# Eight byte offsets for the split halves of the expert blocks in a PEER encoder block

## The chip, the core and the metric

The kernel runs on one core of a Trainium2 chip. Its time is the device time of one execution, in microseconds (us). Five engines work side by side, each through its own instructions in order: TensorE (PE in the rows; PEld is its loading of the stationary operand), VectorE (DVE), ScalarE (ACT), GpSimd (POOL) and SyncE (SP), which here only issues transfers. Transfers (DMA) are issued from the queues of SyncE, ScalarE and GpSimd and are carried by 16 DMA engines. SBUF is the on-chip memory: 128 partitions, each a row of bytes, in which a tile has a start and a length.

## The reference

One encoder layer on 512 tokens of width 1024. The part that matters is the expert stage, in which each token picks 16 of 16384 experts for each of 8 heads, and an expert adds its row of `expert_v`, weighted by a gate and by gelu of its row of `expert_u` times the token:

```python
def peer_block(xb, w_q, sub_keys, expert_u, expert_v):
    T = xb.shape[0]
    q = (xb @ w_q).reshape(T, PEER_HEADS, 2, PEER_HALF)
    s = jnp.einsum('thpd,hpkd->thpk', q, sub_keys)
    sv, si = lax.top_k(s, PEER_TOPK)
...
    top_s, pos = lax.top_k(cand, PEER_TOPK)
    eidx = jnp.take_along_axis(cidx, pos, axis=-1)
    gate = jax.nn.softmax(top_s.astype(jnp.float32), axis=-1).astype(xb.dtype)
    u = jnp.take(expert_u, eidx, axis=0)
    act = jax.nn.gelu(jnp.einsum('thkd,td->thk', u, xb))
    v = jnp.take(expert_v, eidx, axis=0)
    return jnp.einsum('thk,thkd->td', gate * act, v)
```

Before it stands a mixer (input projection, a three-tap convolution and window means, output projection), behind it a gate with a per-layer embedding and the last norm.

## The kernel before

Tokens are handled as four tiles of 128. For three of them (384 tokens) the experts are not gathered but computed densely: all 16384 experts are streamed as 128 blocks of 128, for u and for v. For the fourth tile the chosen rows are gathered one at a time by GpSimd (`fetch`) and worked on by VectorE (lines 559 and 563).

Float32 operands are split in two, since TensorE takes each operand in a rounded 4-byte form (float32r): the high half is the value rounded, the low half is the rest, and a product is three matmuls, high by high, low by high, high by low (`mm3_pair`, lines 126, 128, 130). For a streamed block:

- `u_dma` / `v_dma` (lines 577, 595, SyncE) load 512 KB into `uraw` or `vraw`;
- `u_h` / `v_h` (lines 583, 601, ScalarE) write the high half `uH` or `vH`, `u_l` / `v_l` (589, 607, VectorE) the low half `uL` or `vL`; each of the four names has three buffers of 128 x 1024;
- `score` takes uH and uL as the stationary operand, in 8 slices of 128 columns, against 384 token columns: 24 matmuls a block;
- `mix` takes vH and vL as the moving operand, 512 columns at a time, and the mixing weights `wH` and `wL` (gate times gelu, written by lines 688 and 693 for two blocks at once, in two buffers each) as the stationary one: 18 matmuls a block, into accumulators that stand through all blocks.

The program has three parts in a row. First the mixer and the scores for the top-k. Then 76 blocks of u are scored, while VectorE picks the experts and makes the gate matrix by one-hot products; ScalarE collects that in the tile `stage` (two buffers of 13312 bytes a partition) and stores it to memory from its own queue (line 484), twelve stores of 1664 KB; there a scheduler sets the order of instructions. Last, from about 646 us, comes the mixing, in an order written out by hand: v blocks are mixed in turn, eight of them straight away, then in turn with the 52 blocks of u that are left, then alone. Each engine runs that order; a wait on another engine or on a transfer is put where a tile is first written over bytes that an earlier tile still holds, or is first read. In the mixing, the pools on the left of SBUF lie behind one another: `ub` (uraw, uH, uL), `vb` (vraw, vH, vL), `wq` (the gelu tiles, wH, wL). Pools of the part before lie in the same bytes, `stage` among them.

Of the kernel before, what the change touches and what calls it, by code (L numbers as in the profile page):

```python
# [8 lines left out]
F32R = mybir.dt.float32r  # L9
# [7 lines left out]
P = 128  # L17
T = 512
NT = T // P
D = 1024  # L20
DC = D // P
# [27 lines left out]
GGB = 2  # L49
URB = 2  # L50
G_START = 10
G_RATE1 = 0.7
RATES = (1.5, 3.2, 2.9)
MAIN_ORDER = ((ND, 0, 99), (0, 0, 99), (1, 0, 99), (2, 0, 99))
# [6 lines left out]
def block_kernel(ctx: ExitStack, tc: tile.TileContext, x, pT_in, g_cols, w_in, conv_w, pool_w,  # L61
# [262 lines left out]
    ub = sbx.enter_context(tc.tile_pool(name="ub", reuse_waits="tile", bufs=3))  # L324
# [176 lines left out]
    for hd in range(H):  # L501
# [11 lines left out]
        for tp in range(2):  # L513
            ps = psum.tile([P, T], F32, name="tp", bufs=2)
            for ti in range(2):
                for b in range(2):
                    t = 2 * tp + ti
                    o = (2 * ti + b) * P
# [29 lines left out]
    def gather(n=1, pin=False):  # L548
        for _ in range(n):
            k = done[0]  # L550
            if k >= 2 * P:
                return
            done[0] += 1
            for kk in range(k, min(k + AHEAD_G, 2 * P)):
                if kk not in rows:
                    rows[kk] = fetch(u_rows if kk < P else v_rows, kk % P)
            g = rows[k]
            if k < P:
                ins = nc.vector.scalar_tensor_tensor(g, g, 1.0, xrow, op0=OP.mult, op1=OP.mult,  # L559
                                                     accum_out=act[:, k:k + 1])  # L560
            else:
                accg = accs["g"]
                ins = nc.vector.scalar_tensor_tensor(accg, g, gate3[:, k - P:k - P + 1], accg, op0=OP.mult,  # L563
                                                     op1=OP.add)
            if pin:
                tc.keep_in_program_order(ins)
            if k == P - 1:
                nc.sync.dma_start(xrow, h_d[ND])
                nc.scalar.activation(act, act, AF.Gelu_apprx_tanh)
                nc.vector.tensor_tensor(gate3, gate3, act, op=OP.mult)  # L570

    ublk, vblk, wblk = {}, {}, {}

    def u_dma(i):
        if i < NE:
            raw = ub.tile([P, DC, P], F32, name="uraw", bufs=URB)
            nc.sync.dma_start(raw, u_blk[i])
            ublk[i] = [raw, None, None]

    def u_h(i):  # L580
        if i < NE:
            ublk[i][1] = ub.tile([P, DC, P], F32R, name="uH")
            nc.scalar.activation(ublk[i][1], ublk[i][0], AF.Copy)  # L583

    def u_l(i):
        if i < NE:
            raw, uh, _ = ublk[i]
            ublk[i][2] = ub.tile([P, DC, P], F32R, name="uL")
            nc.vector.tensor_tensor(ublk[i][2], raw, uh.bitcast(F32), op=OP.subtract)  # L589

    def v_dma(n):
# [5 lines left out]

    def v_h(n):
        if n < NE:
            vblk[n][1] = vb.tile([P, D], F32R, name="vH")  # L600
            nc.scalar.activation(vblk[n][1], vblk[n][0], AF.Copy)  # L601

    def v_l(n):
        if n < NE:
            raw, vh, _ = vblk[n]
            vblk[n][2] = vb.tile([P, D], F32R, name="vL")
            nc.vector.tensor_tensor(vblk[n][2], raw, vh.bitcast(F32), op=OP.subtract)  # L607

    def score(ps, i):
# [11 lines left out]
    def prep_u(i):  # L621
        u_dma(i)
        with tc.high_priority(AHEAD):
            u_h(i)
            u_l(i)
# [3 lines left out]
    for i in range(NB):  # L629
# [9 lines left out]
        while mi < len(main) and spent < (i + 1) * total_m / (NB - SLACK):  # L639
            spent += main[mi][0]  # L640
            main[mi][1]()
            mi += 1
        gather(max(0, int((i + 1 - G_START) * G_RATE1) - done[0]), True)
    phg.close()
# [4 lines left out]
    vb = vs.enter_context(tc.tile_pool(name="vb", reuse_waits="tile", bufs=3))  # L649
# [116 lines left out]
    for n in range(3):  # L766
        v_dma(n)
    u_dma(NB + 2)
    u_dma(NB + 3)
    new_quad(0)  # L770
    if NR % 4 == 0:
        new_quad(NR // 4)
    for n in range(2):
        v_h(n)
        w_mult(n)
        w_h(n)
        v_l(n)
        w_l(n)
        v_dma(n + 3)
    heldU = {}  # L780
    for m in range(PRE):
        heldU[m] = acts(NR + m)
        if m == 0:
            for t in range(ND):
                acc[t] = [psum.tile([P, T], F32, name="o%d%d" % (t, hf)) for hf in range(2)]
        u_h(NB + m + 2)
        u_l(NB + m + 2)
        u_dma(NB + m + 4)
        gelu(NR + m, heldU[m])
    LAST = 3  # L790
    left = None
    for n in range(NE - LAST):
        m = n + LAG
        i = n - NS
# [28 lines left out]
        if fu:  # L823
            ps = acts(m)
            u_h(u_of(m) + 2)
# [3 lines left out]
        if fu:  # L829
            u_l(u_of(m) + 2)  # L830
            u_dma(u_of(m) + 4)
        v_h(n + 2)
        if not fu and m < NE:
            w_h(m)
        gather(q >= 2)
        v_l(n + 2)
        v_dma(n + 5)
        if not fu and m < NE:
# [8 lines left out]
        if n == NE - LAST - 1:  # L847
            for k in range(n + LAG + 1, NE):
                w_mult(k)
                w_h(k)  # L850
                w_l(k)
            for k in range(n + 3, NE):
                v_h(k)
                v_l(k)
            tail_norm(ND)
# [145 lines left out]
```

## Time and profile before

| what | us |
|---|---|
| median of three runs | 1451.63 (1448.16 to 1456.77) |
| the profiled execution | 1445.91 |
| its span | 1444.1 |
| TensorE busy | 1423.6 |
| VectorE busy | 1137.7 |
| ScalarE busy | 614.2 |
| GpSimd busy | 383.2 |

The span runs from the first instruction to the last; 1.8 us lie around it. A matmul's busy time overlaps with its neighbour's, so what one costs is read from when they start. Times in the views are counted from the start of the span. An idle time is put down to what ended it.

### The profile page before, as it was taken

The page shows a single profiled execution, that of the slowest core. Times are in us where ns is not written, and L with a number is a line of the kernel's source. Part 1 is how long each engine was busy: PE and PEld are TensorE (multiplying, and loading weights), DVE is VectorE, ACT ScalarE, POOL GpSimd, SP SyncE. Part 2 cuts the span into 40 slices and gives each one's busy share as a digit, 9 for nine tenths or more (in the row PEclk, how much of TensorE's full clock was granted, in tenths as well). Part 3 has the DMA queues.
Part 4 walks back from the last instruction along what each step waited for, and adds up shares of the span by engine and source line. Part 5 has one row for each costly group of instructions (what it writes and reads, how often), then busy time and mean ns, then how long its engine had stood idle before and what let it go on. Part 6 is the DMA issues. An engine that isn't in the chain of part 4 may idle for free.

```text
span 1444.1 us, 20600 instructions
## 1 busy us (share of the span) xinstructions
PE 1423.6 (99%) x7785; PEld 1272.1 (88%) x7785; DVE 1137.7 (79%) x2078; ACT 614.2 (43%) x864; POOL 383.2 (27%) x260
## 2 busy tenths in 40 slices
PE   7999999999998999999999999999999999999997
PEld 5789888999998999998999999999998888888886
DVE  5653579899998997879988778888877777776765
ACT  5321533344564675764333333333332334343345
POOL 0000000002221231125866555444443112332000
PEclk9999999999998999999999999999999999999999
DMA  8233630157788898889998989998987899998621
GB/s 303 88 109 96 235 116 30 34 193 277 226 280 269 286 323 309 281 304 342 390 346 324 374 327 341 348 341 326 342 335 269 320 339 339 339 340 331 249 72 73
DMA packets 152083, 381.38 MB, mean 264 GB/s; under 512 B 10928, under 2 KB 72112, under 8 KB 151728
## 3 DMA queue, kind: packets, MB, share of 16 engines
q1 hardware_dynamic: 72400, 211.75, 40.9%
q0 software_dynamic: 36864, 134.23, 25.4%
q10 hardware_dynamic: 42720, 34.08, 7.0%
q8 instruction: 61, 1.00, 0.3%
q14 instruction: 38, 0.31, 0.1%
HBM read 339.92 MB, written 40.11 MB: 263 GB/s over the span
## 4 chain that ended last, share of the span: by engine, by line
PE 79%; DVE 11%; DMA 6%; ACT 2%; issue 2%; ACTq 0%; SPq 0%; DVEq 0%
PE o L130 11%; PE o L126 11%; PE o L128 11%; PE acc L126 9%; PE acc L130 9%; PE acc L128 9%; PE u L130 5%; PE u L126 5%; PE u L128 5%; DMA uraw<-in_u_blk 3%; DMA tH<-in_w_gate 3%; DVE uL L589 2%; DVE vL L607 1%; PE g L473 1%; PE g L474 1%
## 5 line engine op out<-in xcount | busy, mean ns | idle before, releaser
L539 POOL DMA_INDIRECT gr<-in_u_rows,eidx x128 | 199.5, 1558 | 648.3 <-DVE tsm L393 329.6
L539 POOL DMA_INDIRECT gr<-in_v_rows,eidx x128 | 183.5, 1433 | 289.6 <-DVE xrow L563 278.9
L126 PE MATMUL o<-vH,wH 128*128 128x512 f32 x768 | 237.5, 390 | 0.0
L130 PE MATMUL o<-vH,wL 128*128 128x512 f32 x768 | 237.3, 390 | 0.1
L128 PE MATMUL o<-vL,wH 128*128 128x512 f32 x768 | 236.9, 390 | 0.0
L601 ACT ACTIVATE vH<-vraw 128x1024 fp32r<-128x1024 f32 x128 | 135.5, 1059 | 220.8 <-PE o L130 163.7
L126 PE MATMUL acc<-xH,uH 128*128 128x384 f32 x608 | 206.6, 340 | 3.0 <-ACT uH L583 3.0
L607 DVE TENSOR_TENSOR vL<-vraw,vH 128x1024 fp32r<-128x1024 f32 x128 | 156.2, 1220 | 65.9 <-ACT vH L601 65.9
L128 PE MATMUL acc<-xL,uH 128*128 128x384 f32 x608 | 206.7, 340 | 0.0
L130 PE MATMUL acc<-xH,uL 128*128 128x384 f32 x608 | 204.5, 338 | 0.0
L589 DVE TENSOR_TENSOR uL<-uraw,uH 128x1024 fp32r<-128x1024 f32 x128 | 155.6, 1217 | 25.2 <-ACT uH L583 25.0
L583 ACT ACTIVATE uH<-uraw 128x1024 fp32r<-128x1024 f32 x128 | 135.3, 1058 | 91.4 <-DMA uraw<-in_u_blk 48.8
L130 PEld LDWEIGHTS o<-vH,wL 128*128 128x128 f32 x768 | 144.0, 188 | 31.1 <-DVE wL L693 0.8
L128 PEld LDWEIGHTS o<-vL,wH 128*128 128x128 f32 x768 | 144.2, 188 | 30.8
L563 DVE SCALAR_TENSOR_TENSOR xrow<-gr,gate,xrow 128x1024 f32<-128x1024 f32 x128 | 164.1, 1282 | 5.3 <-DMA xrow<-h_d 4.8
L126 PEld LDWEIGHTS o<-vH,wH 128*128 128x128 f32 x768 | 143.4, 188 | 26.6
L559 DVE SCALAR_TENSOR_TENSOR gr<-gr,xrow 128x1024 f32<-128x1024 f32 x128 | 154.2, 1217 | 2.4 <-DMA gr<-in_u_rows,eidx 2.3
L130 PE MATMUL u<-xH,uL 128*128 128x384 f32 x416 | 139.6, 336 | 0.0
L126 PE MATMUL u<-xH,uH 128*128 128x384 f32 x416 | 139.5, 335 | 0.0
L128 PE MATMUL u<-xL,uH 128*128 128x384 f32 x416 | 139.3, 335 | 0.0
L126 PEld LDWEIGHTS acc<-xH,uH 128*128 128x128 f32 x608 | 115.4, 190 | 3.9 <-ACT uH L583 3.9
L128 PEld LDWEIGHTS acc<-xL,uH 128*128 128x128 f32 x608 | 115.5, 190 | 0.0
(214 smaller groups left out, 2330.7 us busy)
## 6 DMA issues: line engine op xcount, KB each, us to landing
uraw<-in_u_blk SPq DMA_DIRECT2D x128, 512.0 KB, 4.9
vraw<-in_v_rows SPq DMA_DIRECT2D x128, 512.0 KB, 5.8
G_d<-stage ACTq DMA_DIRECT2D x12, 1664.0 KB, 10.4
gq<-G_d SPq DMA_DIRECT2D x26, 768.0 KB, 6.9
A_d<-a ACTq DMA_DIRECT2D x17, 768.0 KB, 5.4
aq<-A_d SPq DMA_DIRECT2D x17, 768.0 KB, 9.3
wraw<-in_w_in SPq DMA_DIRECT2D x8, 1024.0 KB, 5.6
wraw<-in_w_q SPq DMA_DIRECT2D x8, 1024.0 KB, 5.6
```

Of the source, the lines that this page charges most:

```text
L126: nc.tensor.matmul(ps, lh, rh, start=start, stop=False)
L128: nc.tensor.matmul(ps, lh, rl, start=False, stop=False)
L130: nc.tensor.matmul(ps, ll, rh, start=False, stop=stop)
L473: nc.tensor.matmul(o, oh[:, 1, n, :, e], gg[:, 0, n, :, e], start=True, stop=False)
L474: nc.tensor.matmul(o, oh[:, 1, n, :, e], gg[:, 1, n, :, e], start=False, stop=True)
L539: nc.gpsimd.indirect_dma_start(out=g, out_offset=None, in_=table, in_offset=bass.IndirectOffsetOnAxis(ap=eidx[:, k:k + 1], axis=0))
L559: ins = nc.vector.scalar_tensor_tensor(g, g, 1.0, xrow, op0=OP.mult, op1=OP.mult, accum_out=act[:, k:k + 1])
L563: ins = nc.vector.scalar_tensor_tensor(accg, g, gate3[:, k - P:k - P + 1], accg, op0=OP.mult, op1=OP.add)
L583: nc.scalar.activation(ublk[i][1], ublk[i][0], AF.Copy)
L589: nc.vector.tensor_tensor(ublk[i][2], raw, uh.bitcast(F32), op=OP.subtract)
L601: nc.scalar.activation(vblk[n][1], vblk[n][0], AF.Copy)
L607: nc.vector.tensor_tensor(vblk[n][2], raw, vh.bitcast(F32), op=OP.subtract)
```

## The change

Each high and low half of a streamed block becomes a tile of 1024 + 32 elements, of which 1024 are used, from an element that goes by the block's number modulo eight: 0, 1, 2, 4, 8, 12, 16, 24 elements, which are 0, 4, 8, 16, 32, 48, 64 and 96 bytes. Blocks have 128 numbers, so each offset has 16 of them, for u and for v. The loaded blocks (uraw, vraw) and the other tiles start at their pool's usual places.

```diff
+OFFS = (0, 1, 2, 4, 8, 12, 16, 24)
...
+    def moved(pool, name, k):
+        o = OFFS[k % len(OFFS)]
+        return pool.tile([P, D + 32], F32R, name=name)[:, o:o + D]
...
-            ublk[i][1] = ub.tile([P, DC, P], F32R, name="uH")
+            ublk[i][1] = moved(ub, "uH", i).rearrange("p (c n) -> p c n", c=DC)
...
-            ublk[i][2] = ub.tile([P, DC, P], F32R, name="uL")
+            ublk[i][2] = moved(ub, "uL", i).rearrange("p (c n) -> p c n", c=DC)
...
-            vblk[n][1] = vb.tile([P, D], F32R, name="vH")
+            vblk[n][1] = moved(vb, "vH", n)
...
-            vblk[n][2] = vb.tile([P, D], F32R, name="vL")
+            vblk[n][2] = moved(vb, "vL", n)
```

A half's tile has 4224 bytes a partition instead of 4096. There are six such tiles in `ub` and six in `vb`, so `vb` begins 768 bytes further on, and `wq` behind it 1536. The first buffer of wL lay in bytes 137216 to 140288 of a partition, which is the end of the first buffer of `stage` (126976 to 140288); now it lies in 138752 to 141824, across the end of the first and the start of the second (140288 to 153600).

All engines have the same instructions in the same order, and all waits are the same but for two rows of VectorE, at the start of the mixing. Before, they read as follows: the low half of v's first block, the first wL (`a_6386` is the tile of gelu values), the low halves of another block of v and of two blocks of u, a product of gelu and gate, a gather's dot product, and the next vL and wL.

```order
L607 TENSOR_TENSOR vL<-vraw,vH 128x1024 [waits DMAHW4_49,Activation_49]
L693 TENSOR_TENSOR wL<-a_6386,wH 128x768 [waits DMAHW6_49,Activation_49]
L607 TENSOR_TENSOR vL<-vraw,vH 128x1024 [waits DMAHW5_49,Activation_49]
L589 TENSOR_TENSOR uL<-uraw,uH 128x1024 [waits DMAHW7_49,PE_49,Activation_49]
L589 TENSOR_TENSOR uL<-uraw,uH 128x1024 [waits DMAHW0_49,PE_49,Activation_49]
L683 TENSOR_TENSOR a_6386<-a_6386,gres 128x768
L559 SCALAR_TENSOR_TENSOR gr,act<-gr,xrow 128x1024 [waits DMASW6_49]
L607 TENSOR_TENSOR vL<-vraw,vH 128x1024 [waits DMAHW6_49,Activation_49]
L693 TENSOR_TENSOR wL<-a_6386,wH 128x768 [waits DMAHW3_49,Activation_49]
```

The first wL waits on the transfer lane DMAHW6 and the second on DMAHW3; the store of `stage` last issued is the one on DMAHW3. With the change the same rows of VectorE read:

```order
L612 TENSOR_TENSOR vL<-vraw,vH 128x1024 [waits DMAHW4_49,Activation_49]
L698 TENSOR_TENSOR wL<-a_6386,wH 128x768 [waits DMAHW6_49,DMAHW3_49,Activation_49]
L612 TENSOR_TENSOR vL<-vraw,vH 128x1024 [waits DMAHW5_49,Activation_49]
L594 TENSOR_TENSOR uL<-uraw,uH 128x1024 [waits DMAHW7_49,PE_49,Activation_49]
L594 TENSOR_TENSOR uL<-uraw,uH 128x1024 [waits DMAHW0_49,PE_49,Activation_49]
L688 TENSOR_TENSOR a_6386<-a_6386,gres 128x768
L560 SCALAR_TENSOR_TENSOR gr,act<-gr,xrow 128x1024 [waits DMASW6_49]
L612 TENSOR_TENSOR vL<-vraw,vH 128x1024 [waits DMAHW6_49,Activation_49]
L698 TENSOR_TENSOR wL<-a_6386,wH 128x768 [waits Activation_49]
```

The wait on DMAHW3 has moved from the second wL to the first, seven instructions ahead; nothing else differs (line numbers are five higher, since the change adds lines).

## Rows read from the trace of the kernel before

**Rows 1.** The page: the span, and busy time, share of the span and instructions of TensorE.

```profile
span 1444.1 us, 20600 instructions
...
PE 1423.6 (99%) x7785; PEld 1272.1 (88%) x7785; DVE 1137.7 (79%) x2078; ACT 614.2 (43%) x864; POOL 383.2 (27%) x260
```

**Rows 2.** Busy time of the engines in stretches of the mixing: the stretch, its length, then busy us and instructions of each engine, the granted TensorE clock, the share of the DMA engines and GB/s.

```profile
640.00:1180.00 540.00, 540.00 (x2671) 483.89 (x2671) 439.65 (x477) 191.84 (x227) 260.10 (x180) 1.00 0.91 337
1180.00:1385.00 205.00, 204.94 (x906) 169.19 (x905) 150.22 (x155) 82.65 (x95) 50.06 (x26) 1.00 0.85 314
```

**Rows 3.** The timeline of TensorE in the first three mixed blocks: start, length, line, output and operands, shapes, number of matmuls merged in the row. The first block begins at 654.39 us, the third at 662.59 us.

```profile
655.31 0.63 PE L130 MATMUL o<-vH,wL 128*128 128x512 f32 x2
...
659.87 0.62 PE L126 MATMUL o<-vH,wH 128*128 128x512 f32 x2
...
662.59 0.62 PE L126 MATMUL o<-vH,wH 128*128 128x512 f32 x2
663.04 0.62 PE L128 MATMUL o<-vL,wH 128*128 128x512 f32 x2
663.50 0.61 PE L130 MATMUL o<-vH,wL 128*128 128x512 f32 x2
```

**Rows 4.** The timeline of TensorE in a score of the mixing; two matmuls stand between these.

```profile
688.14 0.33 PE L126 MATMUL u<-xH,uH 128*128 128x384 f32 x1
...
688.66 0.33 PE L126 MATMUL u<-xH,uH 128*128 128x384 f32 x1
```

**Rows 5.** The timeline of TensorE in the output projection, where each matmul of 256 columns has a weight load of its own; seven matmuls stand between these.

```profile
128.00 0.28 PE L128 MATMUL acc<-wL,mixH 128*128 128x256 f32 x1
...
128.97 0.28 PE L126 MATMUL acc<-wH,mixH 128*128 128x256 f32 x1
```

**Rows 6.** Groups of instructions on the page: the writing of v's high half by ScalarE and of its low half by VectorE. Columns: line, engine, output and inputs, shapes, number, then busy us and mean ns of one, then idle time before them with what ended most of it.

```profile
L601 ACT ACTIVATE vH<-vraw 128x1024 fp32r<-128x1024 f32 x128 | 135.5, 1059 | 220.8 <-PE o L130 163.7
L607 DVE TENSOR_TENSOR vL<-vraw,vH 128x1024 fp32r<-128x1024 f32 x128 | 156.2, 1220 | 65.9 <-ACT vH L601 65.9
```

**Rows 7.** The instructions of lines 298 and 299, which read the tile zb from its second and from its third element on: ns of one (least, median, most), first and last start.

```profile
L298 DVE SCALAR_TENSOR_TENSOR yb<-zb,cw,yb x4: 750/751/754, 69.3 to 106.6; 128x512 f32<-128x512 f32 x4
L299 DVE SCALAR_TENSOR_TENSOR yb<-zb,cw,yb x4: 744/750/753, 72.1 to 107.4; 128x512 f32<-128x512 f32 x4
```

**Rows 8.** The timeline of VectorE at the start of the mixing: start, length, instruction, and in brackets the idle time before it with what ended it.

```profile
648.88 0.95 DVE L693 TENSOR_TENSOR wL<-a,wH 128x768 fp32r<-128x768 f32 x1
649.76 1.22 DVE L607 TENSOR_TENSOR vL<-vraw,vH 128x1024 fp32r<-128x1024 f32 x1
650.89 1.22 DVE L589 TENSOR_TENSOR uL<-uraw,uH 128x1024 fp32r<-128x1024 f32 x1
653.49 1.22 DVE L589 TENSOR_TENSOR uL<-uraw,uH 128x1024 fp32r<-128x1024 f32 x1 [1.39 <-ACT uH L583]
654.63 0.95 DVE L683 TENSOR_TENSOR a<-a,gres 128x768 f32<-128x768 f32 x1
655.50 1.22 DVE L559 SCALAR_TENSOR_TENSOR gr<-gr,xrow 128x1024 f32<-128x1024 f32 x1
...
656.65 1.22 DVE L607 TENSOR_TENSOR vL<-vraw,vH 128x1024 fp32r<-128x1024 f32 x1
659.72 0.96 DVE L693 TENSOR_TENSOR wL<-a,wH 128x768 fp32r<-128x768 f32 x1 [1.85 <-DMA G_d<-stage]
```

**Rows 9.** The stores of stage to memory: all twelve with their first and last start and their time to landing, then the last one alone (639 to 645 us).

```profile
L484 ACTq DMA_DIRECT2D G_d<-stage x12: 377/377/404, 389.1 to 640.2; - x12
...
DMA to landing us min/median/max: 8.5/10.4/19.4
...
DMA to landing us min/median/max: 19.4/19.4/19.4
```

**Rows 10.** SyncE's queue: its timeline from 645 to 652 us (two loads of v), and what its loads of u and v waited for from 645 to 662 us (total, times, longest).

```profile
648.99 2.33 SPq L595 DMA_DIRECT2D vraw<-in_v_rows  x2
...
SPq L577 <- DMA G_d<-stage: 8.3, 1, 8.3
SPq L595 <- DVE vL L607: 5.5, 2, 3.9
```

**Rows 11.** The same columns as in rows 2, for two stretches in which the last store is under way; the last two are the share of the DMA engines and GB/s.

```profile
651.00:655.00 4.00, 4.00 (x24) 3.91 (x23) 2.62 (x3) 1.47 (x3) 0.00 (x0) 1.00 1.06 404
655.00:658.00 3.00, 3.00 (x15) 2.46 (x14) 2.87 (x4) 1.76 (x3) 1.00 (x1) 1.00 0.97 328
```

**Rows 12.** The same columns, for the two places inside the first 1400 us at which the granted clock falls below 1.

```profile
441.00:444.00 3.00, 1.55 (x18) 1.06 (x16) 2.62 (x5) 1.40 (x2) 0.94 (x1) 1.00 0.94 382
444.00:448.00 4.00, 2.90 (x19) 2.47 (x20) 2.77 (x5) 3.55 (x8) 0.00 (x0) 0.58 1.02 332
448.00:451.00 3.00, 3.00 (x11) 3.00 (x11) 2.93 (x4) 1.43 (x3) 0.00 (x0) 0.50 1.03 327
451.00:454.00 3.00, 3.00 (x18) 3.00 (x17) 2.98 (x4) 0.41 (x1) 0.88 (x1) 0.93 1.08 326
458.00:461.00 3.00, 1.75 (x20) 1.23 (x18) 2.65 (x3) 3.00 (x6) 0.00 (x0) 1.00 0.63 262
461.00:462.00 1.00, 0.76 (x9) 0.59 (x7) 1.00 (x2) 1.00 (x3) 0.00 (x0) 0.84 0.00 0
462.00:465.00 3.00, 3.00 (x10) 3.00 (x10) 3.00 (x5) 1.52 (x3) 0.94 (x1) 0.50 0.53 175
```

## The prediction

> **What bounds the kernel now.** I read the page's busy times first: of a span of 1444.1 us TensorE is busy for 1423.6 us [rows 1]. A mean can hide a stage with another limit, so the busy time by stretches comes next: from 640 to 1180 us TensorE has no idle time at all, from 1180 to 1385 us it has 0.06 us [rows 2]. A TensorE that never waits is bound by its own stream, and a delay put into it at 655 us has 0.06 us of later idle time to disappear in before the tail. So two questions decide: does the change alter what one matmul takes, and does it make TensorE wait anywhere?
>
> For the first, I take starts, not durations, since matmuls overlap. In the timeline of TensorE twelve matmuls of 512 columns start between 659.87 and 662.59 us, one each 227 ns [rows 3]; three of 384 columns take 0.52 us, 173 ns each [rows 4]; eight of 256 columns take 0.97 us, 121 ns each [rows 5]. That is (227 - 121) / 256 = 0.41 ns a column and about 15 ns beside, the same for the three widths and for operands of different pools. Nothing in it looks like two readers in each other's way.
>
> **The change, part by part.** No instruction is added, dropped or moved. What changes is (a) where the halves begin, (b) where the tiles behind them lie, and (c), through (b), one wait.
>
> (a) The halves are written by ScalarE (1059 ns) and VectorE (1220 ns) [rows 6] and read by TensorE: vH and vL as the moving operand (128 blocks x 18 = 2304 matmuls), uH and uL as the stationary one (128 x 24 = 3072). VectorE: the three-tap filter already reads at 4 bytes past its tile's start in line 298 and at 8 in line 299, at 751 and 750 ns [rows 7]; I take 0. ScalarE's writes at such a start have no row; even twice as long they would add 1.06 us per half, and ScalarE has 348 of 540 us free between 640 and 1180 us [rows 2]. I take 0, and that cover is what would have to go first. Stationary operand: at 256 columns a matmul with its own weight load goes by in 121 ns [rows 5], the scores leave 173 ns, so a load may grow by 52 ns unseen; I take 0. Moving operand: no row shows one that starts off its usual place, so it is bounded from both sides. The best: the 15 ns beside the columns vanish in the seven of eight blocks with a new start, 2304 x 7/8 x 15 ns = 30 us less. The worst: blocks 4 bytes off (16 of 128, 288 matmuls of 512 columns) are read at half rate, 288 x 512 x 0.41 ns = 60 us more. I take 0, since the 0.41 ns a column and the 15 ns are the same for every operand in rows 3 to 5, and the one shifted reader that rows show (VectorE) pays nothing.
>
> [...]
>
> (b) Each half grows from 4096 to 4224 bytes. Twelve such tiles put everything allocated after them 1536 bytes further, wL among it.
>
> (c) wL's first buffer now overlaps both buffers of the tile stage, not the first alone. So the first low part of the mixing weights, wL(0), has to wait for the last store of stage; before, the second one, wL(2), did. In VectorE's timeline that store is plain: wL(0) starts at 648.88 us, and wL(2) at 659.72 us after an idle time that "DMA G_d<-stage" ended [rows 8]. The store left at 640.2 us and needed 19.4 us, where the median of the twelve is 10.4 [rows 9].
>
> Now the sum. TensorE wants wL(0) first at 655.31 us, line 130 of the first block [rows 3]. If the store lands as before, wL(0) is done at 659.72 + 0.96 = 660.68 us, and TensorE stands for 660.68 - 655.31 = **5.4 us**. The other end: SyncE's fourth and fifth load of v left from 648.99 to 651.3 us, each after a vL [rows 10]. The vL that releases the second now stands behind wL(0), so its 512 KB no longer share the DMA engines with the store; at 404 GB/s [rows 11] that is 1.3 us sooner, and 4.1 us of stall. I take the middle, **4.7 us**.
>
> Is that all? Queued behind wL(0) on VectorE are vL(1), two uL, a product, a gather's dot product, vL(2) and wL(2). By their starts in rows 8 these take 1.13 + 1.14 + 1.14 + 0.87 + 1.15 + 1.13 = 6.6 us up to wL(2), which would start at 660.6 + 6.6 = 667.2 and end at 668.1 us. TensorE, late by 5.4 us, wants vL(2) at 663.04 + 5.4 = 668.4 and wL(2) at 663.50 + 5.4 = 668.9 us [rows 3]: both are there, by 0.8 us at least, so there is no second stall. SyncE's next loads of u waited 8.3 us for the same store already [rows 10]; nothing new there.
>
> A stall has a second price. [...] Lost: 4 x 0.42 + 3 x 0.50 + 3 x 0.07 = 3.4 us the first time, 1 x 0.16 + 3 x 0.50 = 1.7 us the second. A stall of 4 to 5 us in one piece is more idle time than either had, so I count on a fall, at **2.5 us** (1.7 to 3.4).
>
> Sum: 4.7 + 2.5 = 7.2 us, with bounds 4.1 + 1.7 = 5.8 and 5.4 + 3.4 = 8.8. The profiled execution took 1445.9 us and would take 1453.1. It lies 5.7 us below the median of the three runs, 1451.6, so the forecast for a median is 1451.6 + 7.2 = **1459 us**, 0.5% more. A measurement of this kernel can tell about 0.5%, 7 us, from no change; the forecast stands on that line.
>
> **Rivals.** *The store lands in time.* It has until 655.31 - 0.96 = 654.3 us, 14.1 us after it left; its median sister takes 10.4, and only the slowest 19.4 [rows 9]. Against: the DMA engines are full from 651 to 658 us (shares 1.06 and 0.97 [rows 11]), with nothing in the change to empty them but those 512 KB. Then TensorE never waits and the time is **1451.6 us**, no change.
>
> *TensorE reads a start of 4 bytes at a lower rate.* For it: no row shows such a start, and at 0.41 ns a column TensorE reads nearly three times as fast as VectorE (1220 ns for 1024). Against: VectorE's rows. At half rate, on top of the stall: 1459 + 60 = **1519 us**, slower; it decides from a loss of 25 ns (a tenth) per matmul of those blocks on, 7 us. The profile would have line 126, 128 and 130 matmuls on vH and vL at two speeds.
>
> *A new start helps.* If the 15 ns beside the columns come from tiles that all begin at the same place, seven of eight blocks lose them: 1459 - 30 = **1429 us**. Against: they are the same at 256, 384 and 512 columns and for five different operands [rows 3 to 5].
>
> **How the numbers follow.** Forecast (stall and clock) 0.67, store in time 0.13, slower reads 0.15, a new start helps 0.05. The range leaves out the slower reads and the larger half of the gain, 0.18 together: from 1449 (store in time, less 2.6 of the 3.5 us by which the lowest run before lies under the median) to 1474 us (the upper bound of the sum, 1460.4, the 5.1 us by which the highest run before lies above the median, and slower reads up to a seventh of the price above). Slower by over 0.5%: somewhat over half of the forecast, 0.35, and the slower reads, 0.15: 0.50. Within 0.5%: the rest of the forecast, 0.32, and the store in time, 0.13: 0.45. Faster: 0.05.
>
> **What would show it.** Right: in the changed kernel's VectorE timeline wL(0), not wL(2), has the idle time that a DMA of stage ended, some 9 to 11 us; TensorE has one idle time of 4 to 5.4 us near 655 us; the granted clock falls right behind it; matmuls of 512, 384 and 256 columns keep 227, 173 and 121 ns; VectorE and ScalarE keep their means on the halves. Wrong: matmuls on vH and vL whose spacing depends on the block's number modulo eight (then the reads are at work), no idle time of TensorE near 655 us (then the store was early), or a second idle time behind the first, with wL(2) or a later vL as its end (then VectorE's lead is thinner than 0.8 us).

## The result

The changed kernel takes 1469.9 us (median of four runs, 1467.6 to 1470.6) where the kernel before, measured beside it, took 1449.9 (1446.7 to 1456.8): a ratio of 1.0129, 95% interval 1.0089 to 1.0169, or 18.7 us (12.9 to 24.5). The forecast was 1459, with a range from 1449 to 1474. The profiled execution took 1469.3 us.

The page of the changed kernel: span, and busy time of the engines, to be read against [rows 1].

```profile
span 1467.5 us, 20599 instructions
...
PE 1440.9 (98%) x7785; PEld 1274.5 (87%) x7785; DVE 1137.8 (78%) x2078; ACT 612.8 (42%) x864; POOL 386.5 (26%) x260
```

The span has grown by 23.4 us; VectorE and ScalarE work as long as before, TensorE is busy for 17.3 us more with the same number of matmuls. The stretches of [rows 2], same columns:

```profile
640.00:1180.00 540.00, 536.77 (x2619) 477.02 (x2618) 431.88 (x469) 188.12 (x222) 248.33 (x178) 1.00 0.90 330
1180.00:1385.00 205.00, 202.01 (x857) 160.18 (x857) 146.93 (x145) 77.24 (x88) 63.55 (x28) 1.00 0.86 313
```

Two things show in them. TensorE now has idle time, 3.2 us in the first stretch and 3.0 in the second. And where it is busy it gets less done: 52 matmuls fewer in the same 540 us, of which the idle time and the slow clock behind it, shown next, explain some 24 (4.9 us at 0.2 us each).

**The stall** stands where [rows 3] had three matmuls in a row. TensorE's timeline in the first mixed block of the changed kernel; the bracket gives the idle time and what ended it:

```profile
654.97 0.63 PE L127 MATMUL o<-vH,wH 128*128 128x512 f32 x2
655.43 0.63 PE L129 MATMUL o<-vL,wH 128*128 128x512 f32 x2
659.30 0.84 PE L131 MATMUL o<-vH,wL 128*128 128x512 f32 x2 [3.23 <-DVE wL L698]
659.93 1.06 PE L127 MATMUL o<-vH,wH 128*128 128x512 f32 x2
```

VectorE's timeline shows why, against [rows 8]: the first wL now carries the idle time that a store of stage ended.

```profile
648.22 1.23 DVE L612 TENSOR_TENSOR vL<-vraw,vH 128x1024 fp32r<-128x1024 f32 x1 [2.04 <-ACT vH L606]
658.28 0.96 DVE L698 TENSOR_TENSOR wL<-a,wH 128x768 fp32r<-128x768 f32 x1 [8.84 <-DMA G_d<-stage]
```

Behind it the granted clock falls to half speed, as in [rows 12] (stretches of the changed kernel, columns of [rows 2]):

```profile
659.00:660.00 1.00, 0.70 (x3) 0.55 (x4) 1.00 (x2) 0.00 (x0) 0.00 (x0) 0.89 0.00 0
660.00:663.00 3.00, 3.00 (x9) 2.35 (x8) 3.00 (x4) 0.00 (x0) 0.00 (x0) 0.50 0.52 165
663.00:664.00 1.00, 1.00 (x6) 0.83 (x5) 1.00 (x2) 0.45 (x1) 0.00 (x0) 0.91 0.72 184
```

Lost to the clock: 0.11 + 3 x 0.50 + 0.09 = 1.7 us. So the stall and the slow clock behind it cost 4.9 us of the 23.

**The spacing.** From 1335 to 1380 us both kernels do nothing on TensorE but mixing, without idle time. Its timeline there, first and last row; between their starts lie 199 matmuls in the kernel before (first fence) and 194 in the changed one (second).

```profile
1334.82 0.39 PE L128 MATMUL o<-vL,wH 128*128 128x512 f32 x1
...
1379.93 0.39 PE L130 MATMUL o<-vH,wL 128*128 128x512 f32 x1
```

```profile
1334.84 0.63 PE L131 MATMUL o<-vH,wL 128*128 128x512 f32 x2
...
1379.89 0.40 PE L127 MATMUL o<-vH,wH 128*128 128x512 f32 x1
```

That is 226.7 ns a matmul before and 232.2 now. By all 2304 matmuls of the mixing (start to next start, those over 300 ns left out) it is 227.6 and 232.6. And it goes by the block's number. The changed kernel's timeline at the first matmuls of nine blocks in a row, numbers 112 to 120, whose starts are 0, 4, 8, 16, 32, 48, 64, 96 and again 0 bytes:

```profile
1345.04 0.62 PE L127 MATMUL o<-vH,wH 128*128 128x512 f32 x2
...
1349.19 0.63 PE L127 MATMUL o<-vH,wH 128*128 128x512 f32 x2
...
1353.44 0.62 PE L127 MATMUL o<-vH,wH 128*128 128x512 f32 x2
...
1357.64 0.62 PE L127 MATMUL o<-vH,wH 128*128 128x512 f32 x2
...
1361.79 0.63 PE L127 MATMUL o<-vH,wH 128*128 128x512 f32 x2
...
1365.98 0.62 PE L127 MATMUL o<-vH,wH 128*128 128x512 f32 x2
...
1370.16 0.63 PE L127 MATMUL o<-vH,wH 128*128 128x512 f32 x2
...
1374.30 0.62 PE L127 MATMUL o<-vH,wH 128*128 128x512 f32 x2
...
1378.50 0.63 PE L127 MATMUL o<-vH,wH 128*128 128x512 f32 x2
```

The block of start 4 takes 4.25 us for its 18 matmuls, the one of start 64 takes 4.14. But the block of start 0 takes 4.15 too, where every block before took 18 x 226.7 ns = 4.08. A start alone is therefore not the whole of it; that was the first question for the experiments.

The halves are written as fast as before, against [rows 6] (the changed kernel's page, same columns):

```profile
L606 ACT ACTIVATE vH<-vraw 128x1024 fp32r<-128x1024 f32 x128 | 135.2, 1060 | 218.6 <-PE o L131 183.4
L612 DVE TENSOR_TENSOR vL<-vraw,vH 128x1024 fp32r<-128x1024 f32 x128 | 156.7, 1224 | 70.8 <-ACT vH L606 70.8
```

**Late waits.** What TensorE waited for between 1180 and 1385 us in the changed kernel (engine and line, what it waited for, total us, times, longest); before there was nothing of the kind over 0.06 us.

```profile
PE o L129 <- DVE vL L612: 2.0, 3, 0.7
PE o L127 <- ACT wH L693: 0.4, 2, 0.2
```

With the slow matmuls around these waits they cost 5.9 us, and 0.5 before (counted are the matmuls between 1200 and 1390 us that start over 300 ns after the one ahead, each less 230 ns).

The span's 23.4 us are then: 0.6 until the mixing begins (654.39 to 654.97 us), 2304 x 4.95 ns = 11.4 of spacing, 4.9 of stall and clock, 5.4 of late waits, and 1.1 of the 1248 score matmuls within the mixing, which are 0.9 ns further apart: 23.4 us. Two of these terms are no settled part of the change. The mixing begins between 652.2 and 655.7 us in the traces of the experiments that leave u alone, so 0.6 us can be chance; and the late waits come and go from trace to trace, as the table below shows. Each kernel has one trace.

### The profile page after: what moved, and what is told of

The parts are those of the page before. It is cut to its first block, busy times and chain, and to the rows that moved or that the text cites. A ratio compares the mean times of both kernels' runs of the same rounds, so it can differ in the third digit from the quotient of the medians.

```text
span 1467.5 us, 20599 instructions
## 1 busy us (share of the span) xinstructions
PE 1440.9 (98%) x7785; PEld 1274.5 (87%) x7785; DVE 1137.8 (78%) x2078; ACT 612.8 (42%) x864; POOL 386.5 (26%) x260
## 4 chain that ended last, share of the span: by engine, by line
PE 80%; DVE 9%; DMA 7%; issue 2%; ACT 1%; SPq 0%; another core or an unknown queue 0%; DVEq 0%; ACTq 0%
PE o L127 10%; PE o L131 10%; PE o L129 10%; PE acc L129 10%; PE acc L127 10%; PE acc L131 10%; PE u L129 5%; PE u L131 5%; PE u L127 5%; DMA tH<-in_w_gate 3%; DMA uraw<-in_u_blk 2%; DVE uL L594 2%; DVE vL L612 1%; PE g L474 1%; PE g L475 1%
## 5 line engine op out<-in xcount | busy, mean ns | idle before, releaser
L540 POOL DMA_INDIRECT gr<-in_u_rows,eidx x128 | 192.5, 1504 | 662.2 <-DVE tsm L394 329.7
L540 POOL DMA_INDIRECT gr<-in_v_rows,eidx x128 | 193.9, 1515 | 294.2 <-DVE xrow L564 282.2
L131 PE MATMUL o<-vH,wL 128*128 128x512 f32 x768 | 241.5, 396 | 3.6 <-DVE wL L698 3.2
L129 PE MATMUL o<-vL,wH 128*128 128x512 f32 x768 | 241.8, 396 | 2.0 <-DVE vL L612 2.0
L127 PE MATMUL o<-vH,wH 128*128 128x512 f32 x768 | 242.1, 396 | 0.5 <-ACT wH L693 0.4
L606 ACT ACTIVATE vH<-vraw 128x1024 fp32r<-128x1024 f32 x128 | 135.2, 1060 | 218.6 <-PE o L131 183.4
L612 DVE TENSOR_TENSOR vL<-vraw,vH 128x1024 fp32r<-128x1024 f32 x128 | 156.7, 1224 | 70.8 <-ACT vH L606 70.8
L131 PEld LDWEIGHTS acc<-xH,uL 128*128 128x128 f32 x608 | 114.7, 189 | 1.5 <-DVE uL L594 1.5
```

The source lines that it names most:

```text
L127: nc.tensor.matmul(ps, lh, rh, start=start, stop=False)
L129: nc.tensor.matmul(ps, lh, rl, start=False, stop=False)
L131: nc.tensor.matmul(ps, ll, rh, start=False, stop=stop)
L540: nc.gpsimd.indirect_dma_start(out=g, out_offset=None, in_=table, in_offset=bass.IndirectOffsetOnAxis(ap=eidx[:, k:k + 1], axis=0))
```

## The experiments

Theories, as they stood at the start: *start* (a half that begins off its usual place is read more slowly), *place* (the tiles' new size puts operands of TensorE where they are read more slowly, offset or not), and, as a form of the second, *pair* (what counts is how the starts of the moving and of the stationary operand lie to each other). Results of all runs, beside those of the changed kernel; the spacing is that of 512-column matmuls from 1335 to 1380 us and over the whole mixing, as above; stall + clock is the time by which the matmuls at the stall and right behind it start later than 230 ns after the one ahead, counted like the late waits (so 0.1 us more for the changed kernel than by idle time and clock); the last columns are the ratio to the kernel before (1448.6 to 1449.1 us beside these runs) and what it is in us.

| run | ns 1335-1380 | ns all | stall + clock us | late waits us | ratio (95%) | us |
|---|---|---|---|---|---|---|
| before | 226.7 | 227.6 | 0 | 0.5 | 1 | |
| changed kernel | 232.2 | 232.6 | 5.0 | 5.9 | 1.0129 (1.0089-1.0169) | +18.7 |
| e1 no offset | 231.3 | 231.3 | 3.7 | 2.3 | 1.0136 (1.0119-1.0153) | +19.7 |
| e2 weights 128 | 232.3 | 232.2 | 0 | 2.8 | 1.0068 (1.0037-1.0099) | +9.9 |
| e3 all 128 | 226.7 | 227.4 | 0 | 1.8 | 1.0006 (0.9989-1.0022) | +0.9 |
| e4 wait undone | 232.7 | 232.5 | 0 | 0.6 | 1.0079 (1.0060-1.0099) | +11.4 |
| e5 wait alone | 226.7 | 227.6 | 5.5 | 3.8 | 1.0042 (1.0019-1.0064) | +6.1 |
| e6 four bytes | 236.7 | 236.5 | 6.2 | 1.0 | 1.0158 (1.0139-1.0177) | +22.9 |
| e7 four both | 233.3 | 234.2 | 5.3 | 2.9 | 1.0133 (1.0106-1.0160) | +19.3 |
| e8 turn v | 232.7 | 232.4 | 6.6 | 1.7 | 1.0109 (1.0085-1.0134) | +15.8 |
| e9 turn u | 226.6 | 227.4 | 0 | 3.4 | 0.9997 (0.9983-1.0011) | -0.4 |
| e10 weights 256 | 226.7 | 227.6 | 0 | 1.6 | 0.9999 (0.9981-1.0016) | -0.1 |
| e11 all 64 | 226.7 | 226.7 | 0 | 4.0 | 0.9986 (0.9974-0.9997) | -2.0 |
| e12 all 32 | 226.7 | 227.0 | 0 | 5.6 | 0.9977 (0.9962-0.9992) | -3.3 |

The filler `rpad` at the right end of the memory, where a run changes it, moves stage and its neighbours and so keeps the wait of before, or, in the run of the wait alone, brings the wait of the changed kernel.

**No offset.** The changed kernel with tiles of 4224 bytes and every start at 0.

```diff
-OFFS = (0, 1, 2, 4, 8, 12, 16, 24)
+OFFS = (0, 0, 0, 0, 0, 0, 0, 0)
```

> The changed kernel with all eight offsets set to 0: the halves keep their longer tiles (4224 bytes, so the places of all tiles and the moved wait are those of the changed kernel), but each begins at its tile's start. Start theory (what costs is that the moving operand begins off a tile's start, 4 bytes most): mixing matmuls of 512 columns start every 227 ns again as before the change; what is left is the stall and the clock behind it, about 5 us: 1455 us. Place theory (what costs is that tiles no longer lie at multiples of 4096 bytes to one another; blocks with offset 0 have 231 to 232 ns in the changed kernel too): the mixing matmuls stay at 230 ns or more, 1461 us or more.

1466.5 us, as much as the changed kernel within the intervals (+19.7 and +18.7 us), and 231.3 ns. The start theory falls as the whole cause: 231.3 - 227.6 = 3.7 of the 5.0 ns come without any offset.

**The weights 128 bytes further.** The kernel before; only the relation of wH and wL to vH and vL changes (and the tile of gelu values moves with the weights).

```diff
-    right.tile([P, 504], F32, name="rpad")
+    right.tile([P, 120], F32, name="rpad")
...
+    wq.tile([P, 32], F32, name="wpad", bufs=1)
```

> The kernel before with one filler of 128 bytes ahead of the gelu tiles and the mixing weights, so that wH and wL lie 128 bytes further while vH and vL stay; halves without offsets or longer tiles; the right side moved up by 1536 bytes as in the run with the wait undone, so that no wait moves. Pair theory (what costs is how the starts of the operands that TensorE reads side by side, the moving one and the next stationary one, lie to each other): mixing matmuls slower than 227 ns, 229 to 235, and the time 4 to 15 us above before, 1454 to 1465. Start theory: the moving operands begin where they did, 227 ns and 1450 us.

**All of the mixing 128 bytes further.** The same filler ahead of vraw: v, gelu values and weights move together.

```diff
-    right.tile([P, 504], F32, name="rpad")
+    right.tile([P, 120], F32, name="rpad")
...
+    vb.tile([P, 32], F32, name="vpad", bufs=1)
```

> As the run with the weights 128 bytes further, but the filler stands ahead of the v blocks, so that vraw, vH, vL, the gelu tiles, wH and wL are all 128 bytes further and lie to each other as before. Pair theory: mixing matmuls at 227 ns, 1450 us. Start theory in the form that a start must be a multiple of more than 128 bytes: 229 ns or more and 1455 us or more; in the form that only starts off 16 bytes cost: 227 ns, 1450 us.

The two runs part clearly. The same stretch as above, first and last row: 193 matmuls lie between them with the weights moved alone (first), 199 with all moved (second).

```profile
1334.76 0.39 PE L128 MATMUL o<-vL,wH 128*128 128x512 f32 x1
...
1379.60 0.64 PE L130 MATMUL o<-vH,wL 128*128 128x512 f32 x2
```

```profile
1334.81 0.39 PE L128 MATMUL o<-vL,wH 128*128 128x512 f32 x1
...
1379.92 0.39 PE L130 MATMUL o<-vH,wL 128*128 128x512 f32 x1
```

232.3 against 226.7 ns, +9.9 us against +0.9: 128 bytes between the operands cost, 128 bytes for both don't. Neither run touches a tile's size, an offset or a wait that TensorE feels. For distances of 128 bytes the pair theory holds.

**The wait undone.** The changed kernel with offsets, with the right side moved so that wL(2) waits again.

```diff
-    right.tile([P, 504], F32, name="rpad")
+    right.tile([P, 120], F32, name="rpad")
```

> The changed kernel with the tiles on the right side of SBUF all 1536 bytes higher (the filler at its top is 384 elements shorter), so that the first wL lies inside the first buffer of stage again and the moved wait is back where it was; the offsets stay. If the wait costs what the trace of the changed kernel shows (TensorE idle for 3.2 us at 656 us, and half the clock for 3.4 us behind it, 1.7 us): 5 us less than the changed kernel, 1465 us, no idle time of TensorE near 656 us, and matmuls as in the changed kernel (232.5 ns). If the wait cost nothing in the end: 1470 us.

**The wait alone.** The kernel before with the wait of the changed kernel.

```diff
-    right.tile([P, 504], F32, name="rpad")
+    right.tile([P, 888], F32, name="rpad")
```

> The kernel before with 1536 bytes more of filler at the right end of the memory: no half is moved, no start changed, only the wait on the last store of stage goes from wL(2) to wL(0), as in the changed kernel. Three sizes for this wait are on the table. The prediction's: 7.2 us, so 1456 us against 1448.6. The changed kernel's trace by itself: one idle time of TensorE of 3.2 us and 1.7 us lost to the clock behind it, 4.9 us, so 1453.5. The difference of the changed kernel (1469.9) and the run with the wait undone (1459.4): 10.5 us, so 1459; then the stall must have later idle times in its train, where a late VectorE lets TensorE wait again behind 1230 us. Spacings stay 227 and 174 ns in all three.

Undoing it gives 1459.4 us, 10.5 less than the changed kernel, where 5 were expected; bringing it alone costs 6.1 us (2.8 to 9.3). That leaves two of the three sizes, 4.9 and 7.2, and excludes 10.5. The idle time is the changed kernel's, 3.67 us at the same matmul (its timeline):

```profile
652.61 0.62 PE L128 MATMUL o<-vL,wH 128*128 128x512 f32 x2
656.91 1.02 PE L130 MATMUL o<-vH,wL 128*128 128x512 f32 x2 [3.67 <-DVE wL L693]
```

The 10.5 is a difference of two medians that were not measured side by side. By the ratios to the kernel before, each measured beside its own run, it is 18.7 - 11.4 = 7.3 us, which agrees with 6.1. In the profiled executions the late waits differ besides, 5.9 us in the changed kernel's trace and 0.6 with the wait undone. I took them for a consequence of the stall; the table speaks against it: 5.6 us in its last row, without any stall, 1.0 and 1.7 in two runs with one. They vary from trace to trace, and nothing here ties them to the change.

**Four bytes.** vH and vL at a start of 4 bytes, in tiles of 4608 bytes, which keeps all of them at the same place of 512 bytes; `rpad` is 120, the moved wait comes with it, so the run is compared with the wait alone.

```diff
-            vblk[n][1] = vb.tile([P, D], F32R, name="vH")
+            vblk[n][1] = vb.tile([P, D + 128], F32R, name="vH")[:, 1:1 + D]
...
-            vblk[n][2] = vb.tile([P, D], F32R, name="vL")
+            vblk[n][2] = vb.tile([P, D + 128], F32R, name="vL")[:, 1:1 + D]
```

> As the run of the wait alone, and vH and vL begin 4 bytes into tiles of 4608 bytes, so that all of them stay congruent to each other (512 bytes) and only their relation to the mixing weights is 4 bytes off. The prediction's step (a), that a start costs nothing: the time of the wait alone, 1453 to 1459 us, and 227 ns per matmul of 512 columns. Pair theory (TensorE pays where moving and stationary operand do not begin at the same place of 512 bytes): 232 to 236 ns, 2304 x 4.5 to 8.5 ns = 10 to 20 us on top, 1464 to 1478 us.

**Four bytes for both.** As above, and wH, wL in tiles of 3584 bytes from their second element (wL is written in the same way).

```diff
-            W[n] = [wq.tile([P, 2, TD], F32R, name="wH", bufs=WB // 2), None]
+            W[n] = [wq.tile([P, 2 * TD + 128], F32R, name="wH", bufs=WB // 2)[:, 1:1 + 2 * TD].rearrange("p (i n) -> p i n", i=2), None]
```

> As the run with 4 bytes, and the mixing weights wH and wL begin 4 bytes in as well (tiles of 3584 bytes): every operand of the mixing is off by 4 bytes, their relation is that of before. Pair theory: 227 ns and the time of the wait alone, 1453 to 1459 us. Start theory (a start off a boundary costs by itself, whatever the other operand does): 232 to 236 ns or more and the time of the run with 4 bytes, 1464 to 1478 us.

Here both theories miss half. Again first and last row of the stretch, 191 matmuls with v alone at 4 bytes (first), 192 with all operands there (second):

```profile
1334.68 0.40 PE L130 MATMUL o<-vH,wL 128*128 128x512 f32 x1
...
1379.89 0.40 PE L130 MATMUL o<-vH,wL 128*128 128x512 f32 x1
```

```profile
1334.79 0.63 PE L126 MATMUL o<-vH,wH 128*128 128x512 f32 x2
...
1379.59 0.63 PE L126 MATMUL o<-vH,wH 128*128 128x512 f32 x2
```

236.7 ns, and 233.3 with the relation restored, not 226.7. So a start of 4 bytes for both operands costs by itself, 6.6 ns, and the relation to the weights 3.4 more. Both theories are true in part. Which of the two operands pays for its start of 4 bytes wasn't tried.

**The eight starts on v alone**, in tiles of 4608 bytes, `rpad` 120, with the moved wait.

```diff
+            vblk[n][1] = vb.tile([P, D + 128], F32R, name="vH")[:, OFFS[n % 8]:OFFS[n % 8] + D]
...
+            vblk[n][2] = vb.tile([P, D + 128], F32R, name="vL")[:, OFFS[n % 8]:OFFS[n % 8] + D]
```

> The change's eight starts in turn on vH and vL alone, in tiles of 4608 bytes, so that the tiles themselves stay congruent; uH and uL as before; the moved wait is in it. Pair theory: blocks with a start of 0 keep 227 ns, the seven others pay 3 to 8 ns, 230 to 233 ns in the mean; 1460 to 1470 us. Step (a) of the prediction: 227 ns in all blocks and the time of the wait alone. If the blocks of start 0 are slow too, a matmul also feels its neighbour, or the theory lacks a part.

1463.7 us, 11.0 more than the wait alone (9.7 by the ratios): the starts that the change brings, without its places. First matmuls of the blocks 112 to 115 and 120 to 121 in this run's timeline (starts 0, 4, 8, 16, then 0, 4 bytes):

```profile
1338.72 0.62 PE L127 MATMUL o<-vH,wH 128*128 128x512 f32 x2
...
1342.83 0.64 PE L127 MATMUL o<-vH,wH 128*128 128x512 f32 x2
...
1347.10 0.62 PE L127 MATMUL o<-vH,wH 128*128 128x512 f32 x2
...
1351.26 0.62 PE L127 MATMUL o<-vH,wH 128*128 128x512 f32 x2
...
1372.23 0.62 PE L127 MATMUL o<-vH,wH 128*128 128x512 f32 x2
...
1376.34 0.64 PE L127 MATMUL o<-vH,wH 128*128 128x512 f32 x2
```

Blocks of start 0 take 4.11 us, those of 4 bytes 4.27, of 8 bytes 4.16. In means over all blocks: 228.7 ns at 0; 236.6, 231.7, 231.5, 233.3, 232.9, 231.3 and 233.7 ns at 4, 8, 16, 32, 48, 64 and 96. With the tiles at matching places the blocks of start 0 are nearly back; with the change's places they are not (231.5). None of the seven other starts is a good one; each also puts another distance to the weights, so this run doesn't tell start and distance apart.

**The same on u alone**, in the change's tiles of 4224 bytes (`moved` as in the change), with the wait of before; the edit is against the kernel before.

```diff
-    right.tile([P, 504], F32, name="rpad")
+    right.tile([P, 248], F32, name="rpad")
...
+            ublk[i][1] = moved(ub, "uH", i).rearrange("p (c n) -> p c n", c=DC)
...
+            ublk[i][2] = moved(ub, "uL", i).rearrange("p (c n) -> p c n", c=DC)
```

> The change's tiles of 4224 bytes and eight starts on uH and uL alone (the stationary operand of the scores); the right end of the memory makes room, so that the wait of before stays; all tiles of the mixing shift together by 768 bytes and keep their relation. Prediction's step (a), that a weight load may grow by 52 ns unseen: 174 ns per matmul of 384 columns and 1448 to 1450 us. Place theory in the form left by the runs so far (the scores pay 1.4 ns a matmul in the changed kernel, the mixing pays only for its own operands): 175.2 to 175.5 ns, 3072 x 1.4 = 4 us, 1453 us; the mixing stays at 227 to 228 ns.

1448.0 us, no difference, where I had expected 4 us. The spacing of the scores does grow (175.2 ns over all, 173.9 before), but it reaches the end only in part: the mixing begins 0.6 us later than before and its 1248 score matmuls take 0.9 us more (218.5 for 217.6), 1.5 us, which is inside the interval (to 1.6 us); and 0.6 us in the beginning can be chance, as said above. The mixing stays at 226.6 ns with all of its tiles 768 bytes further.

**Other distances, other common starts.** The kernel before with the weights 256 bytes further (`wpad` of 64 elements), and with everything of the mixing 64 or 32 bytes further (`vpad` of 16 or 8 elements), `rpad` 376 in each.

> The kernel before with the mixing weights wH and wL 256 bytes further and vH, vL where they were; no new wait. It repeats the run with 128 bytes (1457.7 us, 232 ns) at twice the distance. If only distances that are no multiple of 256 bytes cost, 227 ns and 1449 us; if any distance that is no multiple of 512 does, 230 to 233 ns and 1455 to 1461 us.

> The kernel before with all tiles of the mixing (vraw, vH, vL, aq, wH, wL) 64 bytes further, relations kept, no new wait. All of them 128 bytes further cost nothing (1448.9 us); vH, vL, wH and wL 4 bytes further cost 6.6 ns a matmul (234.2). If a start at a multiple of 64 bytes is as good as one at 128: 227 ns and 1449 us. If not: 230 to 234 ns, 1455 to 1464 us.

> The same with 32 bytes. A unit of 32 bytes or less: 227 ns and 1449 us. A unit of 64 bytes: 230 to 234 ns and 1455 to 1464 us, while the run with 64 bytes stays at 1449; a unit of 128 bytes: both slow.

All three stay at 226.7 ns in the stretch from 1335 to 1380 us, where TensorE only mixes, and within 0.5% of the time before. A distance of 256 bytes costs nothing there, and neither do common starts 32 and 64 bytes further. The two common starts are even 2.0 and 3.3 us below the kernel before, 0.1 and 0.2%, and both intervals lie just below 1. A part of it stands in the traces between 690 and 1180 us, where scores and mixed blocks alternate. The first matmul of a mixed block and the first of the score behind it, in the kernel before (first) and with everything 64 bytes further (second):

```profile
907.23 0.63 PE L126 MATMUL o<-vH,wH 128*128 128x512 f32 x2
...
911.35 0.33 PE L126 MATMUL u<-xH,uH 128*128 128x384 f32 x1
```

```profile
905.93 0.61 PE L126 MATMUL o<-vH,wH 128*128 128x512 f32 x2
...
910.01 0.34 PE L126 MATMUL u<-xH,uH 128*128 128x384 f32 x1
```

4.12 against 4.08 us for 18 matmuls. Over all such blocks from 700 to 1000 us it is 228.9 ns before, 228.4 with 128 bytes, 227.2 with 32 and 226.6 with 64. In the kernel before, the first nine matmuls behind a score take 224 to 236 ns and the other nine 227; with 64 bytes all take 226 or 227. The distance to the weights is the same in these four kernels; what differs is where the mixing's operands lie relative to those of the scores. With 64 and 32 bytes the column "ns all" lies 0.9 and 0.6 ns lower than before; over 2304 matmuls that is 2.1 and 1.4 us.

**Two rivals that the traces settle.** The operands' places could matter because ScalarE, VectorE or a transfer touches SBUF at the same time. The mixing matmuls from 1200 to 1384 us during which neither ScalarE nor VectorE has an instruction under way are as slow as the rest: 226.7 ns before, 232.6 in the changed kernel, 232.7 with the weights 128 bytes further, 236.6 with 4 bytes. Those few during which no transfer moves data take 226.6, 232.8, 232.1 and 236.8 ns. So the loss, 5.9 to 6.2 ns in the changed kernel, needs neither work of ScalarE or VectorE nor a transfer.

**Is the distance to its own weights all that a matmul pays for?** In the kernel without offsets 997 of 2241 mixing matmuls lie 128 or 384 bytes off their weights, and the others 0 or 256. At the 232.3 and 226.7 ns that the runs with one distance gave, the mean would be 229.2 ns; it is 231.3. About half of the loss by places, 2.5 of 4.6 ns, is explained by the pair theory; the rest isn't.

## Why the prediction was right in sign and short in size

That the time of 1470 us lies inside the range is luck in good part. The forecast of 1459 had the stall alone, some 6 of the 18.7 us. The rest is a slower TensorE, for which the forecast had nothing; the range reached that far because its upper end added 5.1 us for the spread of the runs and 8.6 for slower reads of the 4-byte blocks. One of the prediction's own signs of being wrong came true: the spacing of the matmuls on vH and vL goes by the block's number, 235.9 ns for the blocks of 4 bytes and 230.3 for those of 64.

**Step (c), the moved wait: right, its size at the lower end.** The wait stands on the instruction that was named, TensorE stands still at the matmul that was named, the clock falls behind it, and no second idle time follows with wL(2) or vL as its end within the next blocks. The sum was 7.2 us (5.8 to 8.8); the trace of the changed kernel has 4.9, the six runs with this wait 3.7 to 6.6, and the time of the wait alone says 6.1 (2.8 to 9.3). The stall was 3.2 us, under its lower bound of 4.1: wL(0) started at 658.28, near the 1.3 us sooner of that bound, and TensorE came 0.6 us later. The bounds of the second price, 3.4 and 1.7 us, are the two falls in [rows 12], each stretch taken by what its clock lacks of 1. Here the fall of the clock cost 1.7, the lower end; it came in five of the six runs with the wait, and in the run without offsets it did not (1.00 behind an idle time of 3.4 us), so it is likely, not certain.

**Step (a), the moving operand: failed.** "I take 0" was wrong: the eight starts on v alone cost 4.8 ns a matmul, 11 us. The reason given was that the 15 ns beside the columns are the same for every operand of [rows 3 to 5]. But in the kernel before every moving and every stationary operand of those rows begins at a multiple of 512 bytes; they could not show what another start does. The second reason, VectorE's 751 and 750 ns at two shifted starts [rows 7], with no unshifted one beside them, says nothing of TensorE. The rest of (a) held: ScalarE and VectorE write at 1060 and 1224 ns, and uH and uL cost 1.6 us at most.

**Step (b), the places: a term left out.** It named the shift of the tiles behind and priced only the wait in it. With no offset at all, tiles of 4224 bytes cost 3.7 ns a matmul, 8.5 us: one buffer of vH or vL then lies 128 bytes off the next, and so 0, 128, 256 or 384 bytes off the weights (modulo 512). Start and place don't add up: 232.4 ns by starts alone, 231.3 by places alone, 232.6 with both. So the 11.4 us by which the changed kernel's spacing grew can't be split between (a) and (b).

**The rivals.** The store did not land in time: wL(0) stood until 658.28 us, after 8.84 us of idle time that the store ended. Matmuls on blocks with a 4-byte start do take longer, but by 9 ns (236.6 against 227.6) and not by the 210 priced; the rival fell as one of those blocks alone, and what made the result is a smaller cost in all blocks. No start gave back the 15 ns; the most was the 2 to 3 us of a common one.

The sum in times: 11.4 us (8.7 to 14.3) with the wait undone and 6.1 (2.8 to 9.3) by the wait are 17.5 of the 18.7 measured.

## What to carry to other kernels

When a change moves a buffer, list where both operands of TensorE begin, before and after. In the stretch where TensorE only mixes, the kernels whose mixing operands all began at one place modulo 256 bytes, at 0, 32, 64 or 128, stayed at 226.6 or 226.7 ns, and the others, at 231.3 to 236.7, lost 2.0 to 4.4%; the scores, with u moved, lost 0.7% (175.2 ns for 173.9). These are the few distances that were tried, not a rule for others. Rows in which all operands share one alignment are no evidence that alignment costs nothing; such a price has to be bounded by what they can't show. And padding a tile by 128 bytes moves all that lies behind it, so the waits by which buffers are handed on have to be read again too.

## What the runs showed of the hardware

- The spacing of fp32r matmuls of 512 columns depends on the distance between the start of the moving operand and that of the stationary one: where TensorE only mixes and all matmuls have the same distance, it is 226.7 ns at distances of 0 and 256 bytes (modulo 512) and 232.3 at 128 bytes. In the rotation on v, with starts and distances of 8 to 96 bytes, it was 231.3 to 233.7 ns.
- A start of 4 bytes for both costs 6.6 ns there (233.3 for 226.7); 32, 64 and 128 bytes for both cost nothing (226.7). Between 4 and 32 bytes no common start was tried.
- The own distance isn't all. With tiles of 4224 bytes and no offset, matmuls whose operands are a multiple of 512 bytes apart also take 230.8 ns; and in the kernel before, the first nine matmuls behind a score take up to 236 ns, and 227 when all of the mixing lies 64 bytes further.
- Which mechanism stands behind it is open. The loss is there in a stretch without idle time (232.2 ns in the changed kernel for 226.7, from 1335 to 1380 us), so it is no wait of the program, and it is there while ScalarE and VectorE rest (232.6 for 226.7) or the transfers do (232.8 for 226.6), so it needs none of them; beyond that only addresses were varied.
